# A hybrid decoder block on one core: the reciprocal square roots of the delta rule and of the second norm, moved from ten VectorE instructions to one GpSimd power each

## The chip, the cores and the metric

One core of a Trainium2 chip runs the whole program in one launch. The metric is device time in microseconds (us), the median of three runs. A core has five engines that work through queues of their own, each strictly in the order in which the program was built: TensorE (PE in the profile, with PEld for its weight loads), VectorE (DVE), ScalarE (ACT), GpSimd (POOL) and SyncE (SP), which issues the DMA transfers. They meet only through semaphores: an instruction that waits for another engine holds up all that stands behind it in its own queue.

## What is computed

One decoder layer over 1024 tokens of width 1024, in float32. An input norm and a wide projection feed two branches: a gated delta rule (8 heads of 128, chunks) and an attention whose keys are selected by a small indexer (the best 256 for each query). The branches are merged by sigmoid gates, projected, added to the input, normed again and sent through a squared-ReLU MLP of width 4096. Cut to what matters here, with the three places at which this case's reciprocal square roots stand:

```python
def rms_norm(x, g):
    return x * lax.rsqrt(jnp.mean(x * x, axis=-1, keepdims=True) + EPS) * g
def l2_normalize(x):
    return x * lax.rsqrt(jnp.sum(x * x, axis=-1, keepdims=True) + EPS)

h = rms_norm(x, norm_mix_g)                      # first norm (not touched)
gq = l2_normalize(silu(conv(q))) * 128 ** -0.5   # per token and head
gk = l2_normalize(silu(conv(k)))                 # "rk" in the kernel
o_gdn = gated_delta_rule_chunked(gq, gk, gv, g, beta)
o_gdn = rms_norm(o_gdn, gdn_norm_g) * silu(z)    # "fo", with q's norm in it
o_att = dsa_sparse_attention(...)
x = x + (sigmoid(gate_a) * o_gdn + sigmoid(gate_b) * o_att) @ w_out
h2 = rms_norm(x, norm_mlp_g)                     # second norm: "nr"
return x + square(relu(h2 @ w_mlp_up)) @ w_mlp_down
```

## The kernel before

**Staging.** The profile's span falls into stages that overlap at their seams: the input norm, the projections of attention and indexer, and the indexer's scores (0 to about 270 us); the delta rule, head by head, with the rest of the input projections as filler on TensorE (to about 850 us); attention and the output projection (to about 1130 us); the MLP (to the end). Nearly all large products are made of three float32r products each (high by high, high by low, low by high), so that TensorE has most of the work. These products into the PSUM tile `dd` are the filler: they wait for few things and are placed wherever TensorE would have nothing else.

**The order of the work** is made when the program is built. Each piece of work is a Python generator; `Weave` (L2371) holds all of them, keeps a clock of its own and at each moment takes the ready one of the best priority. It estimates each instruction's duration by engine and size, and records every instruction through one helper, so that all of them have the line L2499 in the profile. A bare `yield` means that the generator goes on when its last instruction is estimated to be done. The order so found is then fixed on each engine. On GpSimd every `tensor_tensor` is estimated by its size alone, whatever the operation:

```python
if op == "tensor_tensor":
    return wv.issue(name, ins, c["g0"] + n / c["g1"], c["glat"], True)
```

with `g0` of 0.31 to 0.35 us, `g1` of 460 to 488 elements per us and `glat` of 0.2 us, by stage.

**The reciprocal square root** is `rsq_w` (L103): an estimate of the root from the bits of the float, and three Newton steps of three instructions, ten on VectorE, on tiles of 128 x 8 elements or smaller. It writes `rk`, `fo` or `nr` and uses a scratch tile `rkt`, `fot` or `n2t`. With `apart` each of the ten is a separate step of the generator, so that other instructions may come between. The first norm (`norm1`) and the attention's heads (`proj_post`) use it too.

**One head of the delta rule** goes through these steps. `conv` makes k, q and v and clears the first three columns of its tile `cu` by a GpSimd memset. `squares` sums k's squares on ScalarE into `kss` (the profile's tile `ot` holds the rows). `keys` (L1039) makes `es` (decays), `am` (k times k, times decay), and then, from `kss`: `ke` (sum plus epsilon), `rk` (its reciprocal root), `av` and `ck` (root times beta, and times root again), and `am` times `ck`. GpSimd masks `es`. Then `am` goes by DMA through `ZA` into `um`, and GpSimd runs a forward substitution: 31 rows, each a multiply `stmp<-sx,um` and a subtraction `sx<-sx,stmp`, of shapes 128x31 to 128x8x1. The result goes through `ZU` back into `um` (cleared before), `join` (L1186) puts the blocks together (TensorE's `jj`), and `scan` (L1285) walks the eight chunks (TensorE's `cc` and `oo`). `output` (L1339) makes `fe` from the sums of squares, `fo`, and scales the head's result `vv` by it. For every third head the tile `um` is one named `w`.

**The second norm**: `residual` adds the projection to x and sums squares into `nss`; `roots` (L1694) makes `nms` and `nr` for two tokens' blocks at a time three times, then for one, and in `norm2b` (L1947) for the last; the blocks are then scaled by `nr`, combined and transposed by TensorE for the MLP's products, which take sums and differences of blocks made beforehand from the weights (tiles `m`, partly on GpSimd).

Of the kernel before, what the change touches and what calls it, by code (L numbers as in the profile page):

```python
# [9 lines left out]
F32 = mybir.dt.float32  # L10
# [5 lines left out]
OP = mybir.AluOpType  # L16
# [4 lines left out]
P = 128  # L21
S = 1024
D = 1024
NB = S // P
# [26 lines left out]
def body(tc, a, out, dbg=None):  # L51
    nc = tc.nc
    ctx = ExitStack()
    V, A, G, PE, SY = nc.vector, nc.scalar, nc.gpsimd, nc.tensor, nc.sync

    def pool(name, bufs=1, side=None, space=None):
        kw = {}
        if space is not None:
            kw["space"] = space
        elif side is not None:  # L60
            kw["side"] = side
        if space is not DRAM:
            kw["reuse_waits"] = "tile"
        es = ExitStack()
        p = es.enter_context(tc.tile_pool(name=name, bufs=bufs, **kw))
        return p, es
# [13 lines left out]
    padl, padl_es = pool("padl", side="left")  # L80
    ones32 = padl.tile([P, 32], F32, name="padl")
    G.memset(ones32, 1.0)
    cst, cst_es = pool("cst", side="left")
    dr, dr_es = pool("dr", space=DRAM)
    htp, ht_es = pool("htp", side="left")
# [953 lines left out]
    def keys(h):  # L1039
        kt = st[h]["kt"]  # L1040
        if h > 2:
            yield ("scan", h - 3)
        if h > 1:
            yield ("join", h - 2)
        es = gp.tile([P, NB, P], F32, name="es", bufs=3)
        am = gq.tile([P, NB, P], F32, name="am", bufs=2)
        um = slot(3, [P, NB, P], F32) if h % 3 == 2 else gp.tile([P, NB, P], F32, name="um", bufs=2)
        wv.add(3, decayed(h))
        SY_.dma_start(es.rearrange("p b c -> p (b c)"), GC[h:h + 1, :].to_broadcast([P, S]))
        dma = ("es", h)  # L1050
        after(dma)
        yield dma
        for b in range(NB):
            A_.activation(es[:, b, :], es[:, b, :], AF.Abs, bias=ngc[:, b, h:h + 1])
            if b % 2:
                yield
            if b % 4 == 3:
                A_.activation(es[:, b - 3:b + 1, :], es[:, b - 3:b + 1, :], AF.Exp, scale=-1.0)
        yield

        for half in range(2):
            hs = slice(half * 4, half * 4 + 4)
            yield tt.ready
            ps, slot_ = tt.get()
            for i in range(4):
                b = half * 4 + i
                PE_.matmul(ps[:, i, :], blk(kt, b), blk(kt, b), start=True, stop=True)
            yield
            V_.tensor_tensor(am[:, hs, :], ps, es[:, hs, :], op=OP.mult)
            tt.free(slot_)  # L1070
        rk = gp.tile([P, NB], F32, name="rk", bufs=2)
        ke = gp.tile([P, NB], F32, name="ke", bufs=2)
        yield ("kss", h)
        V_.tensor_scalar(ke, st[h]["kss"], 4 * EPS, None, op0=OP.add)
        yield
        yield from rsq_w(gp, rk, ke, NB, "rk")
        ck = gp.tile([P, NB], F32, name="ck", bufs=2)
        av = gp.tile([P, NB], F32, name="av", bufs=3)
        nb_ = gp.tile([P, NB], F32, name="nb", bufs=3)
        yield  # L1080
        V_.tensor_tensor(av, rk, beta[:, :, h], op=OP.mult)
        yield
        V_.tensor_tensor(ck, rk, av, op=OP.mult)
        V_.tensor_scalar(av, av, 0.5, None, op0=OP.mult)
        yield
        V_.scalar_tensor_tensor(nb_, ck, -1.0, eg[:, :, h], op0=OP.mult, op1=OP.mult)
        V_.tensor_tensor(am, am, ck[:, :, None].to_broadcast([P, NB, P]), op=OP.mult)
        for half in range(2):
            hs = slice(half * 4, half * 4 + 4)
            G_.affine_select(es[:, hs, :], es[:, hs, :], pattern=[[0, 4], [1, P]], compare_op=OP.is_ge,  # L1090
                             fill=0.0, base=0, channel_multiplier=-1)
        yield
        st[h].update(aq=es, am=am, av=av, nb=nb_, um=um)
        wv.done("keys", h)

        sx = gq.tile([P, 8, 32], F32, name="sx", bufs=1)
        stmp = gq.tile([P, 8, 32], F32, name="stmp", bufs=1)
        if h:
            yield ("zu", h - 1)
        SY_.dma_start(sx, a["c_xinit"])  # L1100
        for q in range(4):
            SY_.dma_start(ZA[h][:, q].rearrange("n r c -> r n c"),
                          am[32 * q:32 * q + 32, :, 32 * q:32 * q + 32])
        yield
        sa = um.rearrange("p n c -> p (n c)").rearrange("p (r c) -> p r c", r=32)
        for r in range(4):
            SY_.dma_start(sa[32 * r:32 * r + 32], ZA[h].rearrange("n q r c -> (n q) r c"))
        yield
        for j in range(31):
            w, m = j // 4 + 1, 31 - j  # L1110
            G_.tensor_tensor(stmp[:, :w, :m], sx[:, :w, j:j + 1].to_broadcast([P, w, m]),
                             sa[:, j + 1:, j][:, None, :].to_broadcast([P, w, m]), op=OP.mult)
            G_.tensor_tensor(sx[:, :w, j + 1:], sx[:, :w, j + 1:], stmp[:, :w, :m], op=OP.subtract)
            yield
        for r in range(4):
            SY_.dma_start(ZU[h][:, :, r, :], sx[32 * r:32 * r + 32])
        G_.memset(um, 0.0)
        yield
        wv.done("zu", h)
        zu = ZU[h].rearrange("(n q) k r c -> q (k r) n c", q=4)  # L1120
        for q in range(4):
            SY_.dma_start(um[32 * q:32 * q + 32, :, 32 * q:32 * q + 32], zu[q])
        yield
        wv.add(1, join(h))
# [214 lines left out]
    def output(h):  # L1339
        yield ("gate", (h, "a"))  # L1340
        yield ("qss", h)
        if h:
            yield ("out", h - 1)
        oss, qss, oo, og = (st[h][k] for k in ("oss", "qss", "vv", "kt"))
        fo = gp.tile([P, NB], F32, name="fo", bufs=2)
        fe = gp.tile([P, NB], F32, name="fe", bufs=2)
        V_.tensor_scalar(fe, qss, 4 * EPS, 128 * EPS, op0=OP.add, op1=OP.mult)
        yield
        V_.scalar_tensor_tensor(fe, oss, 1.0 / P, fe, op0=OP.mult, op1=OP.add)
        yield  # L1350
        yield from rsq_w(gp, fo, fe, NB, "fo")
        yield
        V_.tensor_tensor(oo, oo, fo[:, :, None].to_broadcast([P, NB, P]), op=OP.mult)
        yield
        if h < H - 1:
            of = oo.rearrange("p b c -> p (b c)")
            yield ot.ready
            og, slot_ = ot.get()
            for half in range(2):
                hs = slice(half * HALF, (half + 1) * HALF)  # L1360
                yield "V"
                V_.transpose(og[:, hs], of[:, hs])
            yield
            dst = TO[h].rearrange("(y i) (r j) -> r i y j", i=32, r=4)
            for r in range(4):
                SY_.dma_start(dst[r], og[32 * r:32 * r + 32].rearrange("p (y j) -> p y j", j=32))
            yield
            ot.free(slot_)
            SY_.dma_start(oo, TO[h].rearrange("(b d) t -> d b t", d=P))
            after(("ol", h))  # L1370
            yield ("ol", h)
            for half in range(2):
                hs = slice(half * HALF, (half + 1) * HALF)
                yield "V"
                V_.scalar_tensor_tensor(of[:, hs], of[:, hs], g025, zzs[h][:, hs], op0=OP.mult, op1=OP.mult)
            yield
            og = of
        else:
            for half in range(2):
                yield tt.ready  # L1380
                ps, slot_ = tt.get()
                for i in range(4):
                    PE_.transpose(ps[:, i, :], oo[:, half * 4 + i, :], ident)
                yield
                hs = slice(half * HALF, (half + 1) * HALF)
                V_.scalar_tensor_tensor(og[:, hs], ps.rearrange("p a b -> p (a b)"), g025, zzs[h][:, hs],
                                        op0=OP.mult, op1=OP.mult)
                tt.free(slot_)
                yield
        SY_.dma_start(M1[h // 4][h % 4], og)  # L1390
        yield
        wv.done("out", h)
# [301 lines left out]
    def roots(tbs, apart=False):  # L1694
        for tb in tbs:
            yield ("ss", tb)
        bs = slice(tbs[0], tbs[-1] + 1, max(1, tbs[-1] - tbs[0]))
        V_.tensor_scalar(nms[:, bs], nss[:, bs], 1.0 / D, EPS, op0=OP.mult, op1=OP.add)
        yield from rsq_w(cst, nr[:, bs], nms[:, bs], len(tbs), "n2", apart=apart)
        yield  # L1700


# [868 lines left out]
```

## Time and profile before

| | |
|---|---|
| time, median of 3 runs | 1750.77 us (1750.61 to 1750.85) |
| the profiled execution's own time | 1751.01 us |
| its span, first to last instruction | 1749.3 us |
| mean granted TensorE clock | 0.999 |
| TensorE busy | 1735.0 us, 99% |
| TensorE weight loads | 1454.3 us, 83% |
| VectorE busy | 1303.6 us, 75% |
| ScalarE busy | 1039.1 us, 59% |
| GpSimd busy | 550.8 us, 31% |
| chain that ended last | TensorE 92%, VectorE 4%, ScalarE 2%, DMA 1% |

The busy times are of the profiled execution and add up over stages with different limits. The time of a run is 1.7 us more than the span, since something lies before the first and after the last recorded instruction. In rows of the trace, the first number is the start in us from the beginning of the span and the second how long the instruction took in us; "x4" is a count of instructions merged into one row; what stands in brackets is the idle time of that engine just before, and what ended it. Shapes are partitions by elements of a partition.

### The profile page before, as it was taken

The numbers are of one execution on the slowest core, as the hardware profiler recorded it, in microseconds if no ns is written. First come the engines' busy times: TensorE is split into PE (matmuls) and PEld (weight loads), VectorE is DVE, ScalarE is ACT, GpSimd is POOL, SyncE is SP. The second block draws the span as 40 slices with busy tenths as digits, with TensorE's granted clock in tenths as the row PEclk, the third lists the DMA queues.
The fourth block names the chain that finished last, engine by engine and source line by source line (L and its number), as shares of the span: only waits on it lengthen the run. The fifth ranks groups of instructions, "written<-read, shape, count | busy, mean of one in ns | idle before, by whom it ended". The sixth has DMA issues, their size and how long they took to land.

```text
span 1749.3 us, 27303 instructions
## 1 busy us (share of the span) xinstructions
PE 1735.0 (99%) x9451; PEld 1454.3 (83%) x9451; DVE 1303.6 (75%) x2510; ACT 1039.1 (59%) x2304; POOL 550.8 (31%) x771
## 2 busy tenths in 40 slices
PE   9999999999999999999999999999999999999999
PEld 7988998888888888888878878888888888888887
DVE  6678668858898898995477686878666677948673
ACT  7466657766677666554467676757666654333331
POOL 0005532552463351734023121313322323722220
PEclk9999999999999999999999999999999999999999
DMA  5631236646787777666474222335444459373341
GB/s 168 156 76 59 85 121 153 146 128 124 170 185 168 167 185 157 144 143 138 122 260 135 70 87 67 109 108 184 160 139 159 160 204 339 122 253 124 96 145 48
DMA packets 441645, 252.15 MB, mean 144 GB/s; under 512 B 234089, under 2 KB 385826, under 8 KB 441506
## 3 DMA queue, kind: packets, MB, share of 16 engines
q1 hardware_dynamic: 441490, 250.41, 51.0%
q8 instruction: 74, 1.21, 0.3%
q14 instruction: 65, 0.53, 0.1%
q10 hardware_dynamic: 16, 0.00, 0.0%
HBM read 169.97 MB, written 80.38 MB: 143 GB/s over the span
## 4 chain that ended last, share of the span: by engine, by line
PE 92%; DVE 4%; ACT 2%; DMA 1%; issue 1%; SPq 0%; DVEq 0%; ACTq 0%
PE dd L2499 55%; PE o L2499 16%; PE s L2499 7%; PE pt L2499 6%; PE cc L2499 2%; PE tt L2499 2%; PE oo L2499 1%; PE sq L2499 1%; PE jj L2499 1%; DVE sc L2499 1%; DVE w L2499 1%; DVE pr L2499 0%; SPq L2499 0%; DMA w<-in_x_dram 0%; ACT hj L2499 0%
## 5 line engine op out<-in xcount | busy, mean ns | idle before, releaser
L2499 PE MATMUL dd<-hh,w 128*128 128x512 f32 x1552 | 505.8, 400 | 0.9 <-DVE w L2499 0.9
L2499 PEld LDWEIGHTS dd<-hh,w 128*128 128x128 f32 x1552 | 286.1, 189 | 52.7 <-DVE w L2499 1.1
L2499 PE MATMUL dd<-hl,w 128*128 128x512 f32 x776 | 312.4, 403 | 0.1
L2499 ACT ACTIVATE m<-m 128x512 f32<-128x512 f32 (+1 forms) x240 | 140.8, 625 | 81.4 <-PE o L2499 34.9
L2499 DVE TENSOR_TENSOR m<-m,m 128x512 fp32r<-128x512 f32 (+2 forms) x184 | 143.1, 807 | 41.7 <-ACT m L2499 36.5
L2499 PEld LDWEIGHTS dd<-hl,w 128*128 128x128 f32 x776 | 146.3, 189 | 27.2 <-DVE hl L2499 1.0
L2499 PE MATMUL dd<-hh,m 128*128 128x512 f32 x504 | 165.4, 393 | 0.3 <-DVE w L2499 0.3
L2499 PE MATMUL dd<-w,hh 128*128 128x256 f32 (+1 forms) x704 | 164.3, 324 | 0.2 <-DVE w L2499 0.2
L2499 POOL TENSOR_TENSOR stmp<-sx,um 128x60 f32<-128x60 f32 (+24 forms) x186 | 81.8, 440 | 162.7 <-DMA um<-ZA 149.4
L2499 PEld LDWEIGHTS dd<-w,hh 128*128 128x128 f32 x704 | 117.9, 190 | 10.0 <-DVE w L2499 0.8
L2499 POOL TENSOR_TENSOR sx<-sx,stmp 128x60 f32<-128x60 f32 (+24 forms) x248 | 109.8, 443 | 19.4
L2499 PE MATMUL dd<-w,hl 128*128 128x256 f32 (+1 forms) x352 | 114.0, 324 | 0.0
L2499 PEld LDWEIGHTS dd<-hh,m 128*128 128x128 f32 x504 | 94.4, 188 | 19.0 <-issue 0.7
L2499 ACT ACTIVATE hh<-m 128x1024 fp32r<-128x1024 f32 x44 | 45.0, 1056 | 98.0 <-PE s L2499 44.6
L2499 DVE TENSOR_SCALAR_CACHE_REDUCE tkeq<-sc,cand 128x384 f16<-128x384 f32 (+3 forms) x128 | 102.9, 804 | 0.5
L2499 PE MATMUL dd<-hl,m 128*128 128x512 f32 x252 | 99.6, 395 | 0.0
L2499 POOL TENSOR_TENSOR m<-m,m 128x512 f32<-128x512 f32 x48 | 65.8, 1379 | 102.1 <-DVE m L2499 53.3
L2499 DVE TENSOR_TENSOR w<-w,w 128x1024 fp32r<-128x1024 f32 (+1 forms) x63 | 70.6, 1120 | 35.0 <-ACT w L2499 30.1
L2499 ACT ACTIVATE ha<-m 128x1024 fp32r<-128x1024 f32 x44 | 45.1, 1055 | 79.3 <-PE s L2499 41.6
L2499 PE MATMUL o<-hh,m 128*128 128x512 f32 x264 | 85.8, 392 | 0.4 <-DVE m L2499 0.4
L2499 POOL TENSOR_TENSOR sg<-sg,m 128x512 f32<-128x512 f32 x16 | 20.9, 1309 | 183.2 <-DVE sg L2499 155.2
L2499 ACT ACTIVATE tkcm<-sc,cand 128x1024 f16<-128x1024 f32 x64 | 73.0, 1141 | 0.6 <-POOL sc L2499 0.2
(428 smaller groups left out, 4416.2 us busy)
## 6 DMA issues: line engine op xcount, KB each, us to landing
HD<-m SPq DMA_DIRECT2D x112, 256.0 KB, 2.3
m<-HD SPq DMA_DIRECT2D x56, 512.0 KB, 3.9
w<-in_w_in_dram SPq DMA_DIRECT2D x48, 512.0 KB, 4.4
m<-in_w_mlp_up_dram SPq DMA_DIRECT2D x33, 512.0 KB, 4.8
m<-in_w_mlp_down_dram SPq DMA_DIRECT2D x16, 512.0 KB, 5.8
w<-in_x_dram SPq DMA_DIRECT2D x10, 512.0 KB, 3.7
wraw<-in_w_in_dram SPq DMA_DIRECT2D x4, 1024.0 KB
es<-GC SPq DMA_DIRECT2D x8, 512.0 KB, 4.8
```

The costliest lines, as they stand in the source:

```text
L2499: ins = f(*args, **kw)
```

## The change

A constant tile of -0.5 is set once. For `rk`, `fo` and the second norm's `nr`, the ten VectorE instructions give way to one GpSimd instruction that raises the sum to the power -0.5. `rsq_w` stays for the first norm and for the attention's heads. Since the planner sees other instructions with other estimates, all that it places after the first `rk` may stand in another order.

```diff
     ones32 = padl.tile([P, 32], F32, name="padl")
     G.memset(ones32, 1.0)
+    mhalf = padl.tile([P, NB], F32, name="mh")
+    G.memset(mhalf, -0.5)
...
         V_.tensor_scalar(ke, st[h]["kss"], 4 * EPS, None, op0=OP.add)
         yield
-        yield from rsq_w(gp, rk, ke, NB, "rk")
+        G_.tensor_tensor(rk, ke, mhalf, op=OP.pow)
...
         V_.scalar_tensor_tensor(fe, oss, 1.0 / P, fe, op0=OP.mult, op1=OP.add)
         yield
-        yield from rsq_w(gp, fo, fe, NB, "fo")
+        G_.tensor_tensor(fo, fe, mhalf, op=OP.pow)
         yield
         V_.tensor_tensor(oo, oo, fo[:, :, None].to_broadcast([P, NB, P]), op=OP.mult)
...
         V_.tensor_scalar(nms[:, bs], nss[:, bs], 1.0 / D, EPS, op0=OP.mult, op1=OP.add)
-        yield from rsq_w(cst, nr[:, bs], nms[:, bs], len(tbs), "n2", apart=apart)
+        yield
+        G_.tensor_tensor(nr[:, bs], nms[:, bs], mhalf[:, :len(tbs)], op=OP.pow)
         yield
```

The order of the built programs shows where the new instruction stands. In the rows below, a name left of the arrow is what is written, names right of it what is read, and a shape the output's. First GpSimd's queue in head 0's substitution. Before, from the pair of shape 5x13 on, its pairs of multiply and subtraction run without a break down to 6x8, and there stands head 1's mask of `es`; the first of these rows:

```order
L2499 TENSOR_TENSOR sx<-sx,stmp 128x5x13
L2499 TENSOR_TENSOR stmp<-sx,um 128x5x12
L2499 TENSOR_TENSOR sx<-sx,stmp 128x5x12
L2499 TENSOR_TENSOR stmp<-sx,um 128x6x11
L2499 TENSOR_TENSOR sx<-sx,stmp 128x6x11
```

and after, in the same queue and place:

```order
L2502 TENSOR_TENSOR sx<-sx,stmp 128x5x13
L2502 TENSOR_TENSOR rk<-ke,mh 128x8
L2502 TENSOR_TENSOR stmp<-sx,um 128x5x12
L2502 TENSOR_TENSOR sx<-sx,stmp 128x5x12
L2502 AFFINE_SELECT es<-es 128x512 x2
L2502 TENSOR_TENSOR stmp<-sx,um 128x6x11
```

Head 1's power has been put into head 0's substitution, and head 1's mask of `es` has come forward from behind the pair of 6x8 to behind that of 5x12. In the same way head 2's power stands in head 1's substitution (behind the row of 4x18), head 3's in head 2's (8x3) and head 7's in head 6's (7x4); those of heads 4, 5 and 6 stand behind the end of a substitution, and head 0's ahead of the first. The powers for `fo` stand where GpSimd has ended one substitution and not yet begun the next.

The second place is VectorE's queue at the last root of the second norm (`norm2b`). Before, ten instructions lead from `nms` to `nr`, of which the first five rows are shown; the last three of these stand three times in all, and then come `w<-w,w`, `m<-m,o` and `hh<-w,nr`:

```order
L2499 TENSOR_SCALAR nms<-nss 128x1
L2499 TENSOR_SCALAR nr<-nms 128x1
L2499 SCALAR_TENSOR_TENSOR n2t<-nr,nms 128x1
L2499 TENSOR_TENSOR n2t<-n2t,nr 128x1
L2499 SCALAR_TENSOR_TENSOR nr<-n2t,nr 128x1
```

After, in the same queue and place, where `nr` comes from GpSimd:

```order
L2502 TENSOR_SCALAR nms<-nss 128x1
L2502 TENSOR_TENSOR m<-m,m 128x512
L2502 TENSOR_TENSOR w<-w,w 128x512
L2502 TENSOR_TENSOR hl<-pt,hh 128x384
L2502 TENSOR_SCALAR hh<-w,nr 128x512
```

Three instructions of other work now stand between the sum and the first that reads the root. On GpSimd this root stands behind `m<-m` and ahead of `m<-m,m`, both 128x4x128 pieces of the MLP's weight sums.

On TensorE the matrix products are the same ones; the first that stand elsewhere are head 0's products of k and q (`tt<-qt,kt`), of which the first four come 15 rows of `dd` products earlier and the next four 21. Up to the first `rk` the order is unchanged on all engines.

## The prediction

> **What bounds the kernel now.** I read the page's first part, then the busy times by stage, then what TensorE waits for, and only then the ten instructions and their neighbours. The first two lines are of the page; the next are the table by stage (busy us and count of PE, PEld, DVE, ACT, POOL, then granted clock, DMA share, GB/s); the last are what TensorE waited for between 800 and 1250 us (us in all, times, longest).
>
> ```profile
> span 1749.3 us, 27303 instructions
> PE 1735.0 (99%) x9451; PEld 1454.3 (83%) x9451; DVE 1303.6 (75%) x2510; ACT 1039.1 (59%) x2304; POOL 550.8 (31%) x771
> 160.00:800.00 640.00, 639.90 (x4040) 542.17 (x4039) 527.58 (x1165) 412.58 (x1152) 280.57 (x583) 1.00 0.63 145
> 800.00:1250.00 450.00, 443.56 (x2342) 368.15 (x2341) 317.30 (x728) 285.39 (x599) 102.83 (x96) 1.00 0.41 129
> 1250.00:1700.00 450.00, 450.00 (x1987) 372.75 (x1986) 323.00 (x375) 226.11 (x338) 143.41 (x62) 1.00 0.51 172
> PE s L2499 <- ACT qh L2499: 1.6, 1, 1.6
> PE s L2499 <- DVE mx L2499: 1.2, 2, 0.7
> PE dd L2499 <- DVE w L2499: 1.2, 2, 0.9
> PE o L2499 <- DVE pl L2499: 1.1, 3, 0.5
> ```
>
> TensorE is the bound from end to end: 1735.0 of 1749.3 us, 14.3 us idle. In the delta rule's stage (160 to 800) it idles 0.1 us of 640, although VectorE is busy 527.6 of these 640 (82%): VectorE is loaded, but TensorE never waits for it. Between 800 and 1250 it idles 6.4 us, of which the three VectorE rows shown make 3.5; the MLP from 1250 on has none. The other 7.8 us are start and tail, which have none of the changed instructions. The change leaves every matrix product in place, so it can win little more than these 3.5 us, or 6.4 with all that is near; it can lose whatever it makes TensorE wait. A change of 0.2% is 3.5 us (0.002 x 1750.8); I take that as what a measurement of this kernel can tell from none.
>
> **What is removed.** 21 roots (8 `rk`, 8 `fo`, 5 `nr`) of ten instructions each, 210. VectorE's time in those that touch the scratch tiles, by the table by stage for one tile each (`rkt`, `fot`, `n2t` in this order), and the last two roots as they ran:
>
> ```profile
> 160.00:900.00 740.00, 12.75 (x72) 1.00 0.62 147
> 160.00:900.00 740.00, 11.78 (x72) 1.00 0.62 147
> 900.00:1250.00 350.00, 8.13 (x45) 1.00 0.37 120
> 870.58 0.17 DVE L2499 TENSOR_SCALAR fo<-fe 128x8 int32<-128x8 int32 x1
> 872.60 1.22 DVE L2499 TENSOR_TENSOR vv<-vv,fo 128x1024 f32<-128x1024 f32 x1
> 1133.68 0.15 DVE L2499 TENSOR_SCALAR nr<-nms 128x1 int32<-128x1 int32 x1
> 1134.06 1.15 DVE L2499 TENSOR_TENSOR n2t<-n2t,nr 128x1 f32<-128x1 f32 x1
> 1136.48 0.68 DVE L2499 TENSOR_TENSOR w<-w,w 128x512 f32<-128x512 f32 x1
> ```
>
> 12.75 + 11.78 + 8.13 = 32.7 us for 189 instructions, and 21 estimates of 0.17 each are 3.6: 36 us of VectorE, 3% of its 1303.6. Where nothing comes between, ten of them take 2.0 us from the estimate to the first reader (870.58 to 872.60), 2.8 at the last norm (1133.68 to 1136.48). Of this, `rk` and `fo` have 27 us (24.5 and 16 estimates), nearly all in the delta rule's stage, where TensorE idles 0.1 us: worth nothing there. The cover is the `dd` products; were it gone, the chain of a head would count, and would be 2 us or more shorter.
>
> **What is added.** 21 powers on GpSimd and one memset at the start. The trace has no power. Its bounds are these groups (busy us, mean ns of one, then idle before): the smallest two-input operation, the same shape read in strides, and the mean of all subtractions.
>
> ```profile
> L2499 POOL TENSOR_TENSOR sx<-sx,stmp 128x8 f32<-128x8 f32 x8 | 1.8, 220 | 0.6
> L2499 POOL TENSOR_TENSOR stmp<-sx,um 128x8 f32<-128x8 f32 x6 | 4.1, 691 | 0.3
> L2499 POOL TENSOR_TENSOR sx<-sx,stmp 128x60 f32<-128x60 f32 (+24 forms) x248 | 109.8, 443 | 19.4
> ```
>
> Below, it cannot be cheaper than the 0.22 us of the same shape. Above, I bound it by ten such operations, as many as the root has now: 10 x 0.443 = 4.4 us. I take 0.7, the dearer of the two rows of the same shape, since a power has more to do than a subtraction. GpSimd has room: 21 x 0.7 = 15 us beside 550.8. What matters is where it stands, since GpSimd now waits in the middle of a head's substitution for VectorE's `ke` of the next.
>
> **The wait in head 0's substitution.** The rows are GpSimd's pair 5x13 and its end, ScalarE's last sum, VectorE's `ke`, SyncE's issues and TensorE's first `jj`:
>
> ```profile
> 323.02 0.30 POOL L2499 TENSOR_TENSOR sx<-sx,stmp 128x65 f32<-128x65 f32 x1
> 334.82 0.22 POOL L2499 TENSOR_TENSOR sx<-sx,stmp 128x8 f32<-128x8 f32 x1
> 328.10 0.19 ACT L2499 ACTIVATION_READ_ACCUMULATOR ot<-ot 128x1 f32 x1
> 328.32 0.40 DVE L2499 TENSOR_SCALAR ke<-kss 128x8 f32<-128x8 f32 x1 [1.69 <-ACT ot L2499]
> 338.58 2.60 SPq L2499 DMA_DIRECT2D ZU<-sx  x4
> 343.10 1.81 SPq L2499 DMA_DIRECT2D um<-ZU  x4
> 351.94 0.45 PE L2499 MATMUL jj<-um,am 32*32 32x32 f32 x32
> DMA to landing us min/median/max: 1.8/1.9/1.9
> ```
>
> GpSimd is through 5x13 at 323.3 and `ke` of head 1 is there at 328.7. The hand-over is short (the sum ends at 328.29, `ke` starts at 328.32); I take 0.1. With 0.7 the substitution goes on at 329.5 instead of 323.3: 6.2 us later, end 335.0 + 6.2 = 341.2. `ZU` was issued at 338.58, behind other transfers, so it moves by 2.6 + 0.1. `um` lands (343.10 + 1.81 + 1.9 = 346.8, the last line being issue to landing of these four) 2.7 later at 349.5, before `jj` at 351.94. TensorE waits only from a power of 0.7 + 2.4 = 3.1 us on. Behind GpSimd's wait stand the rest of the substitution, the mask of head 1 (itself needed after `ke`) and a memset of `cu`; on SyncE, behind `ZU`, the input weights, which move by the same 2.7.
>
> **The wait in head 6's substitution**, for head 7's `ke`:
>
> ```profile
> 730.83 0.24 POOL L2499 TENSOR_TENSOR sx<-sx,stmp 128x28 f32<-128x28 f32 x1
> 734.43 0.22 POOL L2499 TENSOR_TENSOR sx<-sx,stmp 128x8 f32<-128x8 f32 x1
> 741.02 0.16 DVE L2499 TENSOR_SCALAR ke<-kss 128x8 f32<-128x8 f32 x1
> 742.38 2.52 SPq L2499 DMA_DIRECT2D ZU<-sx  x4
> 748.93 2.15 SPq L2499 DMA_DIRECT2D um<-ZU  x4
> 757.28 0.31 PE L2499 MATMUL jj<-um,am 32*32 32x32 f32 x13
> DMA to landing us min/median/max: 3.8/3.8/3.8
> ```
>
> From 7x4 (ends 731.07) to the end (734.65) are 3.6 us, now begun at 741.2 + 0.8 = 742.0: end 745.6, `ZU` 3.3 later. `um` (748.93 + 2.15 + 3.8 = 754.9) lands at 758.2 and `jj`, at 757.28, waits 0.9. That is the only place where I find TensorE waiting; but `ke` itself, freed of earlier roots on VectorE, may come as much earlier. I take +0.4, half of it. The waits of different heads do not add: once TensorE is late by one, every later wait has that much more room. The other two waits inside a substitution are those of heads 1 and 2, for the `ke` of the first and third rows; the second and fourth are their `ZU`.
>
> ```profile
> 382.08 0.16 DVE L2499 TENSOR_SCALAR ke<-kss 128x8 f32<-128x8 f32 x1
> 406.50 2.52 SPq L2499 DMA_DIRECT2D ZU<-sx  x4
> 462.90 0.13 DVE L2499 TENSOR_SCALAR ke<-kss 128x8 f32<-128x8 f32 x1
> 468.67 1.86 SPq L2499 DMA_DIRECT2D ZU<-sx  x3
> ```
>
> In head 0, the twelve pairs behind 5x13 took 11.7 us, 1.0 each. Head 1 has 17 pairs left at 382.2 + 0.8 = 383: 400, ahead of 406.5. Head 2 has two at 463.8: 466, ahead of 468.67. No cost. Heads 4 to 6 find GpSimd between substitutions, and so do all `fo`, whose latency falls from 2.0 to 0.7 + 0.2.
>
> **The second norm.** Five roots of 2.0 to 2.8 us become 0.9. Where other work stands between, VectorE waits nothing. The 8 us saved are 2.5% of VectorE's 317.3 in that stage; of the 3.5 us of TensorE's waits for VectorE I give back a tenth, -0.4.
>
> Against it, the row of 1134.06 took 1.15 us for 128 x 1: it ends as this one of GpSimd does (1135.19), and the two share something.
>
> ```profile
> 1133.87 1.32 POOL L2499 TENSOR_TENSOR m<-m 128x512 f32<-128x512 f32 x1
> ```
>
> The Trainium skill, page "SBUF — State Buffer", section "SBUF: two separate sides", says that a VectorE operation with two SBUF inputs and a GpSimd one exclude each other over one pair of ports, the later one waiting for the whole of the earlier. By that rule, with which these two rows agree, a power may wait up to the 1.3 us of a VectorE operation on 128 x 1024; at 2.0 us a power, head 6's wait would be 0.9 + 1.3 = 2.2 instead of 0.9 and the sum 1752; I keep the row's 0.7, since such meetings are some of 21.
>
> **Sum**: +0.4 - 0.4 = 0, against the profiled execution's 1751.01 (span 1749.3 and 1.7 around it), which is 0.24 above the median of 1750.77. Prediction 1750.8.
>
> **Rivals.** (1) *The power is slow* (slower, the other side of mine): at 4.4 us head 6's wait is 0.9 + 3.7 = 4.6 us, and the last root takes 4.4 + 0.2 against 2.8, some +1.8 on a chain that ends in TensorE's transposes: 1757. It passes 3.5 us from a power of about 3.3 on (0.9 + 2.6). For it: nothing excludes a power that is worked out in steps; against it: the shape is tiny. (2) *The new order is worse*: it is planned with a power at a multiply's price, everything from the first `rk` on is placed anew, and the 6.4 us that TensorE idles between 800 and 1250 are all of such origin. Doubled they give 1757. Against it: only 0.1 us of idle time in 640 arose in the stage where most of the change lies. (3) *The new order is better*: VectorE's 36 us free the waits for it, and its 3.5 us and part of the rest vanish: 1746 to 1747. For it: VectorE is at 82% there; against it: only five roots stand in the stage with idle time. (4) *The change does not do what it says*: VectorE, freed of 36 us, waits as long for GpSimd's answer; then TensorE sees nothing, the same 1751, and it lies in my forecast.
>
> **How the numbers follow.** Forecast within 3.5 us of now, 0.68; slow power 0.11; worse order 0.09; better order 0.12. Below 1747 lies most of the better order, 0.09, and above 1756.5 half of the two worse ones, 0.10: range 1747.2 to 1756.5. Faster by over 0.2% 0.12, within 0.68, slower 0.20.
>
> **What would show it.** Right: 210 fewer VectorE instructions and about 36 us less of its time; 21 powers `rk<-ke`, `fo<-fe`, `nr<-nms` near 0.7 us; TensorE's busy time still 1735 and idle 14 to 15; GpSimd idle some 6 us before the power in head 0's substitution and 10 in head 6's. Wrong: powers of 3 us and more, TensorE waiting at `jj` in the delta rule, or 10 us and more of idle time between 800 and 1250.

## The result, and the profile after

The changed kernel takes **1767.29 us** (median; 1766.46 to 1767.61) against 1750.81 of the kernel before: a ratio of 1.0093, 95% interval 1.0076 to 1.0111. That is 16.5 us slower, and outside the predicted 1747.2 to 1756.5. The profiled execution of the changed kernel took 1767.61 us.

First the changed kernel's page and its table by stage (columns as in the prediction):

```profile
span 1765.9 us, 27103 instructions
PE 1751.9 (99%) x9451; PEld 1450.9 (82%) x9451; DVE 1276.3 (72%) x2300; ACT 1042.3 (59%) x2304; POOL 584.6 (33%) x793
160.00:800.00 640.00, 639.63 (x4001) 533.64 (x4000) 510.06 (x1017) 408.55 (x1136) 311.49 (x600) 1.00 0.62 145
800.00:1250.00 450.00, 444.11 (x2332) 364.29 (x2331) 303.08 (x656) 285.49 (x600) 105.54 (x96) 1.00 0.40 125
1250.00:1700.00 450.00, 450.00 (x1966) 368.52 (x1965) 313.27 (x372) 227.48 (x347) 137.51 (x63) 1.00 0.50 172
```

TensorE's idle time is what it was: 1765.9 - 1751.9 = 14.0 us against 14.3. Its **busy** time grew from 1735.0 to 1751.9, by 16.9 us, with the same 9451 matrix products at the same granted clock of 1.00. The loss is therefore in the products' own pace, not in TensorE's waits. The count in the last row shows it where none of the changed instructions runs: in 450 us of the MLP, busy without a gap both times, TensorE starts 1966 products instead of 1987. And not all products are slower. Two groups of the list by line, operation and tile (busy us, mean ns of one), before:

```profile
L2499 PE MATMUL dd<-hh,w 128*128 128x512 f32 x1552 | 505.8, 400 | 0.9 <-DVE w L2499 0.9
L2499 PE MATMUL pt<-ha,ha 128*128 128x512 f32 x56 | 21.8, 389 | 0.0
```

and after:

```profile
L2502 PE MATMUL dd<-hh,w 128*128 128x512 f32 x1552 | 514.8, 404 | 0.0
L2502 PE MATMUL pt<-ha,ha 128*128 128x512 f32 x56 | 21.8, 389 | 0.0
```

The names behind the arrow are the operand that streams (moving) and the one that is loaded (stationary). `hh` with `w` lost 9 us. `ha` with `ha`, a product of the same shape, lost nothing. That is the clue: `hh` and `ha` are tiles of the left side of SBUF, `w` of the right. The powers themselves came out so (count, shortest, median and longest in ns; then whom GpSimd waited for ahead of them, and how long the reader of the root waited for it, us in all and times):

```profile
L2502 POOL TENSOR_TENSOR rk<-ke,mh x8: 1636/1642/2692, 283.7 to 747.5; 128x8 f32<-128x8 f32 x8
L2502 POOL TENSOR_TENSOR fo<-fe,mh x8: 1635/1642/2609, 410.4 to 869.6; 128x8 f32<-128x8 f32 x8
L2502 POOL TENSOR_TENSOR nr<-nms,mh x5: 558/710/933, 989.2 to 1140.9; 128x2 f32<-128x2 f32 x3, 128x1 f32<-128x1 f32 x2
  DVE ke L2502: 91.5, 7
  POOL rk L2502: 5.3, 6
  POOL fo L2502: 8.2, 6
```

A power of 128x8 takes 1.64 us, not 0.7, and VectorE waited 13.5 us for such roots. But TensorE's waits between 800 and 1250 us name no root; they sum to 5.7 us, and the three longest are for other tiles than before:

```profile
PE dd L2502 <- POOL hl L2502: 2.5, 3, 1.4
PE s L2502 <- DVE qlo L2502: 1.3, 3, 0.6
PE s L2502 <- DVE hl L2502: 0.8, 1, 0.8
```

### The profile page after: what moved, and what is told of

It reads as the page before. It is cut to its first block, busy times and chain, and to the rows that moved or that the text cites. A ratio compares the mean times of both kernels' runs of the same rounds, so it can differ in the third digit from the quotient of the medians.

```text
span 1765.9 us, 27103 instructions
## 1 busy us (share of the span) xinstructions
PE 1751.9 (99%) x9451; PEld 1450.9 (82%) x9451; DVE 1276.3 (72%) x2300; ACT 1042.3 (59%) x2304; POOL 584.6 (33%) x793
## 4 chain that ended last, share of the span: by engine, by line
PE 92%; DVE 4%; DMA 1%; ACT 1%; issue 1%; SPq 0%; POOL 0%; DVEq 0%; ACTq 0%; POOLq 0%
PE dd L2502 55%; PE o L2502 16%; PE s L2502 7%; PE pt L2502 6%; PE cc L2502 2%; PE tt L2502 2%; PE oo L2502 2%; PE sq L2502 1%; PE jj L2502 1%; DVE sc L2502 1%; DVE w L2502 1%; SPq L2502 0%; DMA w<-in_x_dram 0%; DMA XD<-w 0%; DMA m<-M 0%
## 5 line engine op out<-in xcount | busy, mean ns | idle before, releaser
L2502 PE MATMUL dd<-hh,w 128*128 128x512 f32 x1552 | 514.8, 404 | 0.0
L2502 DVE TENSOR_TENSOR m<-m,m 128x512 fp32r<-128x512 f32 (+2 forms) x184 | 139.5, 789 | 45.4 <-ACT m L2502 40.3
L2502 POOL TENSOR_TENSOR sx<-sx,stmp 128x60 f32<-128x60 f32 (+24 forms) x248 | 116.9, 471 | 19.4
L2502 PEld LDWEIGHTS dd<-w,hl 128*128 128x128 f32 x352 | 66.3, 188 | 4.8
```

The source lines that it names most:

```text
L2502: ins = f(*args, **kw)
```

## The experiments

**Theories.** *Placement*: the diff does one thing besides the roots. Its tile `mh`, 8 columns of float32, is 32 bytes on the left side of SBUF, ahead of nearly everything there. The addresses in the built programs (bytes in a partition, two tiles for many):

```
              hh0 (left)   w0 (right)   w0 - hh0
before          4064         221152      217088 = 848 x 256
after           4096         221152      217056 = 848 x 256 - 32
```

`hh`, `hl`, `ha`, `la` and three of the tiles `m`, which lie on the left, moved by 32; `w` and the other tiles `m` did not. *Power*: the 1.64 us of each power and its waits cost the time. *Order*: the newly planned order does. The ratio given with each run is against the kernel before, timed again beside it (medians of 1750.5 to 1750.8 us).

**1. The 32 bytes without the powers**, in the kernel before:

```
-    ones32 = padl.tile([P, 32], F32, name="padl")
+    ones32 = padl.tile([P, 40], F32, name="padl")
```

> The kernel before with its unused first tile widened by 32 bytes: no power, the same instructions in the same order, but hh, hl, ha, la and the others of the left side's first part stand 32 bytes further on, as in the changed kernel. Placement theory (the products slow down since their operands stand at other addresses): about 1767 us, TensorE busy about 1752, VectorE still 1303 in 2510 instructions. Power theory (the 1.64 us of each power and its waits cost the time) and order theory (the new order of instructions costs it): about 1751 us, TensorE busy 1735.

Measured: 1766.68 us, ratio 1.0093 (1.0078 to 1.0108).

```profile
span 1765.2 us, 27303 instructions
PE 1751.7 (99%) x9451; PEld 1452.3 (82%) x9451; DVE 1302.6 (74%) x2510; ACT 1039.8 (59%) x2304; POOL 551.0 (31%) x771
1250.00:1700.00 450.00, 450.00 (x1966) 368.61 (x1965) 314.33 (x373) 226.81 (x346) 143.20 (x63) 1.00 0.51 172
```

The instructions of the kernel before (27303, 2510 of VectorE), and the slowness of the changed one: 1751.7 us busy, 1966 products in the MLP's stretch.

**2. The powers without the 32 bytes**, in the changed kernel:

```
-    G.memset(ones32, 1.0)
-    mhalf = padl.tile([P, NB], F32, name="mh")
-    G.memset(mhalf, -0.5)
+    G.memset(ones32, -0.5)
+    mhalf = ones32[:, :NB]
```

> The changed kernel with all 21 powers, but the exponents are the first 8 columns of the unused first tile, so that no tile is added and hh, hl, ha, la stand where they stood before. Placement theory: TensorE busy about 1735 and 1749 to 1752 us in all. Power theory and order theory: about 1767 us as in the changed kernel, TensorE busy about 1752.

Measured: 1750.25 us, ratio 1.0001 (0.9992 to 1.0010).

```profile
span 1750.4 us, 27102 instructions
PE 1735.5 (99%) x9451; PEld 1453.7 (83%) x9451; DVE 1276.9 (73%) x2300; ACT 1041.1 (59%) x2304; POOL 589.3 (34%) x792
  POOL rk L2501: 5.8, 6
  POOL fo L2501: 8.2, 6
```

All 21 powers are there, VectorE waits 14.0 us for them, and the time is that of the kernel before. Runs 1 and 2 together settle the cause: the loss is the 32 bytes. The powers and the new order, taken together, cost and bring nothing that can be measured.

**3. 128 bytes instead of 32.** The changed kernel with `mh` of 32 columns:

```
-    mhalf = padl.tile([P, NB], F32, name="mh")
+    mhalf = padl.tile([P, 32], F32, name="mh")     # and [:, :NB] of it
```

> The changed kernel with an exponent tile of 128 bytes instead of 32: hh, hl, ha, la stand 128 bytes further on than before, so at the same place within a line of 128 bytes (96) but not within 4096 bytes. If placement counts by 128 bytes or less: TensorE busy about 1735, 1749 to 1752 us. If it counts by a longer period (4096 bytes, say), or if the powers or the order are the cause: about 1767 us.

Measured: 1764.29 us, ratio 1.0083 (1.0066 to 1.0099), TensorE busy 1748.5. So a place that repeats every 128 bytes is not the rule. The longer period that I had in mind, 4096, is not it either, as the next three show.

**4. Products alone, 32 pairs of places.** A micro kernel that computes nothing of the reference: one loaded tile, products of 128x128 by 128x512, each pair of places on a source line of its own.

```
PE.matmul(ps, STAT(112, ops(n)[0]), MOV(0, ops(n)[1]), ...)   # stationary 112, moving 0
```

> Products of 128x128 by 128x512 in the three-product pattern of the dense stages and nothing else on the chip, 48 for each of 32 pairs of places: stationary operand at 0, 16, ... 112 bytes, moving operand at 0, 32, 64, 96 bytes, past a multiple of 128. Placement theory, if it lies in TensorE's own reading: pairs differ by 2 to 4 per cent, the pair (96, 96) at about 0.225 us for one product and (0, 96) at 0.233. If it lies in contention with the other engines' reading and writing, or if placement is not the cause: all pairs alike within 0.5 per cent.

The groups by line went from 11.0 to 11.4 us for 48, and neither operand's own offset sorted them. The pair (96, 96), for which I had expected the fast pace, took 11.4; the fastest was (112, 0):

```profile
L119 PE MATMUL ps<-mv,st 128*128 128x512 f32 x48 | 11.4, 395 | 0.0
L122 PE MATMUL ps<-mv,st 128*128 128x512 f32 x48 | 11.0, 389 | 0.0
```

The two tiles began 4224 bytes apart, 128 past a multiple of 256, so the fast pair is the one nearest to a distance of 0 (112 - 128 = -16). That gave the next run its form.

**5. The distance between the two operands.** The same with tiles that begin a multiple of 512 bytes apart, and the distance as the variable:

> Products of 128x128 by 128x512 alone on the chip again, 48 for each pair of places. Now the stationary operand stands 0, 16, ... 496 bytes further on than the moving one (counted in 512 bytes), with the moving one at one place; eight of these distances again with the moving operand 352 bytes further on; and one stationary and one moving tile alone at distances over 2048 bytes. If the distance between the two operands sets the pace (what the 32 pairs of the first grid point to): distance 0, as in the kernel before, about 10.8 us for 48 (0.225 us each), 32 and 128 about 11.3 (0.235), the same with the moving operand elsewhere; and the third part shows whether the distance counts within 512 bytes or beyond. If each operand's own place counts: the second part differs from the first. If traffic of the other engines is needed: all alike.

Groups of 48 by line; the distances (stationary minus moving) are, in this order, 0, 16, 32, 128, 192 and 256, then 0 and 64 with the moving operand 352 bytes further on:

```profile
L38 PE MATMUL ps<-mv,st 128*128 128x512 f32 x48 | 11.0, 389 | 0.0
L41 PE MATMUL ps<-mv,st 128*128 128x512 f32 x48 | 11.1, 389 | 0.0
L44 PE MATMUL ps<-mv,st 128*128 128x512 f32 x48 | 11.4, 395 | 0.0
L62 PE MATMUL ps<-mv,st 128*128 128x512 f32 x48 | 11.4, 395 | 0.0
L74 PE MATMUL ps<-mv,st 128*128 128x512 f32 x48 | 11.2, 391 | 0.0
L86 PE MATMUL ps<-mv,st 128*128 128x512 f32 x48 | 11.0, 389 | 0.0
L134 PE MATMUL ps<-mv,st 128*128 128x512 f32 x48 | 11.1, 390 | 0.0
L137 PE MATMUL ps<-mv,st 128*128 128x512 f32 x48 | 11.4, 395 | 0.0
```

At the two places of the moving operand that were tried only the distance counts, and it counts modulo 256 bytes: at 0 and up to 16 either way 11.0 to 11.1 us, at 176 and 192 11.2, elsewhere 11.3 to 11.4. The third part of the run had the same values at distances of 512, 1024 and 1536 more. A wrong distance costs (11.4 - 11.05) / 48 = 7 ns a product, 3%, with no other engine at work. No number in this run needs contention with VectorE or a DMA.

**6. The distance restored otherwise.** If the distance counts, the changed kernel can keep its 32 bytes on the left, provided that the right side moves too:

```
+    padr, padr_es = pool("padr", side="right")
+    G.memset(padr.tile([P, 56], F32, name="padr"), 1.0)
     w8, w8_es = pool("w8", side="right")
```

> The changed kernel as it is, with its 32 bytes on the left side, and 224 unused bytes added at the start of the right side, which move w, m and the rest of the right side down by 224: left and right are then 256 bytes further from each other than before, and hh begins at 4096 as in the changed kernel. If the distance of the two operands counts, by a period of 256 bytes: TensorE busy about 1736, 1750 us. If the place of hh itself counts: busy about 1752 and 1767 us, as in the changed kernel. If the period is longer than 256 bytes: about 1767 too.

Measured: 1750.54 us, ratio 0.9999 (0.9990 to 1.0008).

```profile
PE 1735.8 (99%) x9451; PEld 1453.8 (83%) x9451; DVE 1276.7 (73%) x2300; ACT 1040.9 (59%) x2304; POOL 589.5 (34%) x794
1250.00:1700.00 450.00, 450.00 (x1987) 372.64 (x1986) 322.49 (x378) 226.22 (x339) 138.88 (x61) 1.00 0.51 171
```

`hh` begins at 4096, as in the slow kernel, and the 1987 products are back. In the whole kernel, too, what counts is the distance and not the place: 32 less (the change) and 128 less (run 3) are slow, 256 less is at the old pace.

**7. Whose stationary operand.** TensorE loads the next product's stationary operand while this one's moving operand streams (the loads are the row PEld, 83% busy beside a PE at 99%). In products of two kinds in turn, the distance to the own and to the next one's stationary operand can differ:

> Products alone on the chip. First part, 96 products of 128x128 by 128x512 of two kinds in turn: apart from their own stationary operand by 0 while the next one's stands 96 or 160 off, and the other way round. If the pace is lost where the next product's stationary operand is loaded while this one's moving operand streams: the first of these slow (22.7 us for 96), the second fast (22.1). If a product's own two operands count: the reverse. Second part, 256 and 128 columns in place of 512, and 128 columns of plain float32, at eight distances: if the loss is one of the load beside the stream, it is about 6 ns for each product also at 256 columns; at 128 columns and in plain float32 there is no number to go by.

Groups by line: 96 products with own and next distance 0; own 0 and next off; own off and next 0; both off; then 0 and 0 once more, at the end of the run; then 256 columns at distances 0, 32, 96 and 128:

```profile
L43 PE MATMUL ps<-mv,st 128*128 128x512 f32 x96 | 21.9, 389 | 0.0
L47 PE MATMUL ps<-mv,st 128*128 128x512 f32 x96 | 22.6, 396 | 0.0
L51 PE MATMUL ps<-mv,st 128*128 128x512 f32 x96 | 22.3, 392 | 0.0
L55 PE MATMUL ps<-mv,st 128*128 128x512 f32 x96 | 22.7, 396 | 0.0
L163 PE MATMUL ps<-mv,st 128*128 128x512 f32 x96 | 22.1, 390 | 0.0
L67 PE MATMUL ps<-mv,st 128*128 128x256 f32 x96 | 11.7, 283 | 0.0
L71 PE MATMUL ps<-mv,st 128*128 128x256 f32 x96 | 11.5, 281 | 0.0
L79 PE MATMUL ps<-mv,st 128*128 128x256 f32 x96 | 11.4, 280 | 0.0
L83 PE MATMUL ps<-mv,st 128*128 128x256 f32 x96 | 11.7, 283 | 0.0
```

Most of the loss goes with the **next** product's operand: with it alone off, 22.6 is nearly the full 22.7. But the own operand has a part: with it alone off 22.3, against 21.9 and 22.1 with both at 0 (the two mixed cases repeated within 0.1). The expectation, which gave the loss to one of the two, was too simple. My 6 ns at 256 columns was wrong: there distances 0, 128 and 160 took 11.7 us and the other five 11.4 to 11.5, so that 0 is slower than 32 by 2 ns a product. At 128 columns all eight distances took the same, 21.6 us for 192 float32r products and 10.9 for 48 of plain float32 (two rows each in the trace).

The whole kernel shows the same. Run 1 has the products of the kernel before in the same order, so the two traces can be laid side by side, from one product's start to the next one's, with the distances by the addresses. The 3746 float32r products of 512 columns (each with another float32r product behind it) for which both distances were 0 and both became wrong take 4.3 ns more on average, 16.1 us in all; the 49 with only the next one wrong 4.9 ns, the 81 with only their own 2.3; the 1995 that kept both at 0 0.4 ns. 660 of 256 columns take 1.8 ns less, 1.2 us in all. So some 15 of the 16.7 us of run 1 lie in the products whose distances changed.

Why a wrong distance costs time stays open; the runs give the period and the price, not the part. The Trainium skill, page "TensorE: Matmul & The Clock Gate", section "Step-by-step: what each phase is for", says that TensorE reads the two operands through ports of their own, so that loading the next weights takes no read bandwidth from the running product. The runs here differ: at distances of 96 and 160 from the next operand, with no other engine at work, 96 products take 22.6 us instead of 21.9 to 22.1, so loading the next weights is not free at every distance; whether it is read bandwidth that is lost, the run does not say. The measurement decides.

**8. Each power twice**, at the old place, to see how near a slow power is to costing something:

```
         G_.tensor_tensor(rk, ke, mhalf, op=OP.pow)
+        G_.tensor_tensor(rk, ke, mhalf, op=OP.pow)      # fo likewise
```

> The kernel with the powers at the old place (second experiment), and each of the 16 powers of rk and fo issued twice, which lengthens them from 1.64 to some 3.3 us; the second has the same result. If the power lies beside TensorE's products and its length costs nothing: within 0.1 per cent of the second experiment, about 1750.3 us. If it stands on the path to the next head's products: 16 times 1.64 us more, some 1776 us, or a part of it, to be seen as TensorE idle.

Measured: 1761.32 us, ratio 1.0063 (1.0046 to 1.0080). My first expectation fell. The page, two of TensorE's waits, and VectorE's waits for the two roots:

```profile
span 1759.6 us, 27135 instructions
PE 1737.5 (99%) x9451; PEld 1452.4 (83%) x9451; DVE 1273.4 (72%) x2300; ACT 1041.2 (59%) x2304; POOL 626.4 (36%) x808
PE dd L2503 <- DVE w L2503: 4.3, 3, 3.1
PE cc L2503 <- DVE sst L2503: 3.0, 3, 1.6
  POOL rk L2503: 16.6, 8
  POOL fo L2503: 15.8, 7
```

VectorE's waits grow from 14.0 to 32.4 us, and TensorE's idle time from 14.9 to 22.1, the longest in waits for VectorE's tiles (`w`, `sst`: 0.7 and 0.4 in run 2). The order is planned anew as well, so it is not shown how many of the 11 us are the longer power's; run 10 bears on that.

**9. The planner told the power's price**, at the old place:

```
+            if kw.get("op") == OP.pow:
+                return wv.issue(name, ins, 0.33 + 0.164 * n, c["glat"], True)
             if op == "tensor_tensor":
                 return wv.issue(name, ins, c["g0"] + n / c["g1"], c["glat"], True)
```

> The powers at the old place, and the planner that sets the order is told that a power of n elements takes 0.33 + 0.164 n us (1.64 for 128x8) instead of the 0.35 that it takes any operation of GpSimd of that size for. If orders planned from the wrong price cost waits: up to 2 us less than the second experiment, about 1748.5 us. If TensorE's own time bounds the kernel wherever the power stands: 1750.3 us within 0.1 per cent, TensorE busy 1735.

Measured: **1747.67 us**, ratio 0.9984 (0.9974 to 0.9993): the fastest version, and the first that beats the kernel before, by less than the 3.5 us that the prediction took as the least to be told, though the interval leaves out 1. VectorE now waits 1.2 us for `fo` and not for `rk`; TensorE:

```profile
PE 1732.1 (99%) x9451; PEld 1453.1 (83%) x9451; DVE 1275.3 (73%) x2300; ACT 1037.7 (59%) x2304; POOL 587.4 (34%) x792
```

With a span of 1745.8 that is 13.7 us idle, 1.2 less than in run 2, and 3.4 us less busy. Part of this is the one execution that was profiled: run 2's took 1752.19 us, 1.9 over its median, run 9's 1747.56. Why the rest is gained in this order was not found.

**10. Priced at twice what it takes** (0.33 + 0.328 n). In the texts put on record for runs 10 to 12, "the sixth experiment" is run 9, and "third micro run" is run 7:

> The powers at the old place, priced at twice what they take (0.33 + 0.328 n us). If the gain of the sixth experiment comes from orders that put other work ahead of a slow power: about 1747 to 1748.5 us here too, since a later use costs nothing while TensorE has work. If it was a chance of that one order: anywhere within 1746 to 1754 us.

Measured: 1757.91 us, ratio 1.0036 (1.0022 to 1.0049); span 1756.2, TensorE busy 1735.6, so 20.6 idle. The expectation that a late use costs nothing was wrong for this order: VectorE waits 0.6 us for the roots, but what stands behind them comes later (the last `rk` begins at 753.8 us, at 738.0 in run 9), and TensorE idles 6.9 us more than in run 9, in the attention (`s` for `mx` 1.7 us, `pt` for `pr` 1.4 from ScalarE; `s` for `qh` 2.3, where run 9 has 2.0). That the one makes the other was not tested.

**11. The kernel before in another order**: the planner's price for a small VectorE operation 0.16 instead of 0.17.

> The kernel before, no power, with the planner's price of a small VectorE operation set to 0.16 instead of 0.17 us, which gives another order of the same instructions from the middle of the program on. It shows how far the time moves by a change of order alone: within 0.1 per cent (1749 to 1752.5 us) if the gain of 3 us in the sixth experiment is more than the scatter between orders; 3 us or more either way if it is within that scatter.

Measured: 1750.56 us, ratio 0.9998 (0.9989 to 1.0007). A change of order alone does not move the time by 3 us in this one case; two draws more of this kind would be needed to call the gain of run 9 one of the right price and not of one lucky order. Runs 2, 9 and 10, at 0.35, 1.64 and 2.95 us for a power that takes 1.64, have the best time at the true price, with one order each.

**12. The last wrong distances.** By the addresses, 216 products of 512 columns still stream in run 9 while a stationary operand of the delta rule, 32 bytes off, is loaded. One scratch tile widened by 32 bytes puts them right:

```
-            junk = gp.tile([P, P], BF16, name="gj")
+            junk = gp.tile([P, P + 2 * NB], BF16, name="gj")[:, :P]
```

> The priced kernel (sixth experiment), with one scratch tile widened by 32 bytes, so that the delta rule's stationary operands (kt, qt, um, es, kd, am) too stand a multiple of 256 bytes from w. Before this, 216 products of 512 columns stream while the next one's stationary operand stands 32 bytes off; now none of these is left. If the load of the next stationary operand sets the loss (third micro run): 216 times 6 ns, 1.3 us less than the sixth experiment, about 1746.4 us. If a product's own operands set it: no change, 1747.7.

Measured: 1748.07 us, ratio 0.9983 (0.9974 to 0.9991), TensorE busy 1732.5. The 1.3 us did not show; they are within the interval's half of 1.5, so the times leave it open. The traces of runs 9 and 12 have the same order and can again be laid side by side: the products put right (215 by their rows) take 2.9 ns less each, give or take 0.5, so 0.6 us in all. Their own distances were 0 before and after, so this is the next one's part alone, at half the price expected. Drift between the two executions hides it in the total: the 5877 float32r products of 512 columns whose distances were 0 both times took 0.3 ns more each, 1.8 us.

## Why the prediction was wrong, point by point

**The step that failed** is the one that I did not work out: "The change leaves every matrix product in place, so it can win little more than these 3.5 us, or 6.4 with all that is near; it can lose whatever it makes TensorE wait." The products stayed in their places in the program, not in memory, and a product's duration was taken as fixed. The sum counted the added tile as "one memset at the start" and gave it no price. Its price is 16.4 to 16.9 us of TensorE's busy time (run 1 with the 32 bytes alone 16.7, the change against run 2 16.4, against the kernel before 16.9), more than all the terms that were weighed. By the addresses in the built programs, 288 products of 512 columns had the next stationary operand at a distance other than a multiple of 256 before, 3906 after. 16.9 us over these 3618 is 4.7 ns each, and 4.3 by the products laid side by side (run 7), against 7 ns in the micro kernels. The 684 products of 256 columns give back some 1.2 us of it; why the rest of the kernel loses less for each stays open. "TensorE's busy time still 1735" was the line that showed it at once. No rival had it: all four asked what waits.

**The bound** was right: TensorE idles 14.0 us after and 14.3 before. VectorE lost 1303.6 - 1276.3 = 27.3 us where I had 36, and not a microsecond of it shows in run 2. The 36 was a sum of durations, and rows of VectorE overlap: added up one by one they went from 1440.9 to 1403.8 us, 37.1 less, but a stretch that two rows cover is busy only once.

**The power** was mis-sized: 0.7 us taken, 1.64 measured for 128x8, and 0.56 to 0.93 for the two columns or one of the second norm. The range of 0.22 to 4.4 held it. To go by the row of the same shape failed, since that row was another operation. The rival of a slow power was nearer; that a power is worked out in steps, its reason, is not shown by any run.

**The wait in head 0's and head 6's substitution** is there as predicted: GpSimd idles 4.6 us in the one (5.4 by the rows of the prediction) and 16.2 in the other (10), where run 2, at the old pace of the products, has 16.1:

```profile
324.18 1.65 POOL L2502 TENSOR_TENSOR rk<-ke,mh 128x8 f32<-128x8 f32 x1 [4.61 <-DVE ke L2502]
747.50 2.61 POOL L2502 TENSOR_TENSOR rk<-ke,mh 128x8 f32<-128x8 f32 x1 [16.17 <-DVE ke L2502]
747.33 1.28 DVE L2502 SCALAR_TENSOR_TENSOR t<-cu,vecs,t 128x1024 f32<-128x1024 f32 x1
693.97 1.64 POOL L2502 TENSOR_TENSOR fo<-fe,mh 128x8 f32<-128x8 f32 x1 [6.74 <-DVE fe L2502]
694.76 1.28 DVE L2502 SCALAR_TENSOR_TENSOR qt<-cu,vecs,qt 128x1024 f32<-128x1024 f32 x1 [0.88 <-ACT qt L2502]
```

No `jj` waits for it: of the +0.4 at head 6 nothing came, and the -0.4 of the second norm is too small for these runs to tell, so that the sum of 0 was met in run 2 without either term being borne out. The second row also answers the rule weighed in the prediction (the Trainium skill, "SBUF — State Buffer", section "SBUF: two separate sides": GpSimd's and VectorE's two-input operations exclude each other). This power took 2.61 instead of 1.64 us, 0.97 more, beside a VectorE operation of 1.28 us that had begun 0.17 earlier. So far the trace agrees with the rule; three of the sixteen `rk` and `fo` were lengthened so, each begun 0.1 to 0.17 us after such a VectorE operation. The other way round it does not: the VectorE operation of the last row, also with two inputs in SBUF, began 0.79 us into a power, and both took their usual time. The measurement decides.

**The rivals.** (1) *Slow power*: at 1.64 us it costs nothing (run 2); at twice that, run 8 loses 11 us, where I had 3.5 us from 3.3 us on. 7.2 of the 11 are idle time of TensorE, in waits for VectorE's tiles above all and none at `jj`; the order planned anew has a part that was not told apart. (2) *Worse order*: run 10 shows that an order planned from a wrong price can lose 7 us; the one made here, with a price that was too low, lost none. (3) *Better order*: not in the change, but run 9 gained 3.1 us, somewhat less than the 3.8 to 4.8 I gave it, by an order planned with the true price; whether the price or that one order did it is open (run 11). (4) *Nothing happens*: in run 2, where the bytes do not move, TensorE sees nothing, at 1750.25 us, 0.55 from the forecast. VectorE waits 14.0 us there for the powers, about half of the 26.7 it is freed of, and not as long as this rival had it.

## What to carry to other kernels

A tile of 32 bytes can cost more than the instructions that it serves: when a change adds or drops a tile, compare the addresses of the operands of the products that bound the kernel, and try the change once at the old addresses before judging it. When TensorE's busy time moves and its idle time does not, look at the operands and not at the waits. And give a planner that sets the order the measured price of a new operation: the same 21 powers stood at 1747.7, 1750.3 and 1757.9 us with a price that was right, too low and too high, though with one order for each, so this is a lead and not a proof.

## What was not expected of the hardware

- Products of 512 columns of float32r run at 0.229 us each (11.0 us for 48) when the loaded operand and the streaming one stand a multiple of 256 bytes apart, within 16 bytes, and at up to 0.2375 (11.4) elsewhere. At the two places tried the addresses themselves didn't matter, and the loss goes mostly with the operand loaded for the next product (22.6 us for 96 with that one off, 22.3 with the own one off, 22.7 with both, 21.9 to 22.1 with none).
- At 256 columns the distances fall otherwise and differ less (11.7 us for 96 at 0, 128 and 160, 11.4 to 11.5 at the others tried); at 128 columns there is no difference (21.6 us for 192).
- A power on GpSimd takes 1.64 us for 128x8, 0.56 to 0.93 for one or two columns, and 2.6 to 2.7 for 128x8 where it begins just behind a VectorE operation of 1.28 us with two inputs in SBUF.
